# One-hot gates for eight tokens at a time, all on VectorE, with the stationary operand written token by token

## The chip, the cores and the metric

The kernel runs on one core of a Trainium2 chip. A core has engines that run beside one another, each with its own queue: TensorE (PE in the profile; its weight loads are PEld), VectorE (DVE), ScalarE (ACT), GpSimd (POOL) and SyncE (SP, which issues DMAs). The metric is the device time of one execution in microseconds (us). Three runs of the kernel before took 3183.05, 3179.83 and 3183.05 us; the median is 3183.05. [...]

## The reference

Two layers over 512 columns (256 latent tokens and 256 context tokens of 1024 features). Each layer has a mixer (a chunked gMLP in the first, a bidirectional S5 in the second) and then PEER, a layer of 16384 experts with one neuron each. The change touches PEER alone:

```python
def block(hb):                                   # 128 tokens
    q = (hb @ w_q).reshape(PEER_BLOCK, PEER_HEADS, 2, PEER_DHALF)
    s = jnp.einsum("nhkd,hkmd->nhkm", q, sub_keys)
    s_half, i_half = lax.top_k(s, PEER_TOPK)     # 16 of 128 keys, in both halves
    cand = s_half[:, :, 0, :, None] + s_half[:, :, 1, None, :]
    top_s, top_c = lax.top_k(cand.reshape(PEER_BLOCK, PEER_HEADS, 256), PEER_TOPK)
    k1 = jnp.take_along_axis(i_half[:, :, 0], top_c // PEER_TOPK, axis=-1)
    k2 = jnp.take_along_axis(i_half[:, :, 1], top_c % PEER_TOPK, axis=-1)
    ids = k1 * PEER_KEYS + k2
    g = jax.nn.softmax(top_s, axis=-1)
    act = jax.nn.gelu(jnp.einsum("nd,nhkd->nhk", hb, jnp.take(u_tab, ids, axis=0)))
    return jnp.einsum("nhk,nhkd->nd", g * act, jnp.take(v_tab, ids, axis=0))
```

So each token picks 8 heads x 16 = 128 experts (k1, k2), each with a gate g.

## The kernel before

PEER is not computed by gathering rows, but for the last 128 tokens of layer 0. For the other tokens (384 in layer 0, 256 in layer 1) the products with all 16384 experts are made, in 128 chunks of 128 experts, and the activations are multiplied by a matrix of gates that is zero where an expert was not chosen. A *front* (`front`, L695 on) loads a chunk of the U table, splits it into a high and a low part (`split`, L292: the high part on ScalarE, L296; the low part on VectorE or GpSimd, L298; tiles `uh` and `ul`), makes 24 TensorE products (L304 to L306) and applies GELU (L708). A *back* does the like with the V table.

The gate matrices are made by `gate_units` (L626), 128 tokens at a time, called a block below: three blocks in layer 0, two in layer 1. The 128 picks of a token lie on the 128 partitions after a transpose. For a group of 4 tokens VectorE compares a table of the numbers 0 to 127 (`iot`, each number four times, once per token) with the picks' k2 (L664, giving `o2`) and k1 (L666, giving `eq`), and multiplies `eq` by the gates. A gate is a sum of two float16 numbers, so there are two such products in `o1`: the upper one is made by VectorE (L668), the lower one (L669) by the engine `second`, which is GpSimd but for the third block of layer 0, where it is VectorE. In the tiles a token is the last index, so that a token's 128 places lie 8 bytes apart. TensorE then makes for each token o2^T times both halves of o1 (L653 and L654, two products with 128 stationary and 128 moving columns, both sides read in steps of 8 bytes), ScalarE copies a bank of four tokens to `Gs` (L655), and every 16 tokens a DMA writes 1 MB to DRAM, which the backs read.

There are 384/4 + 256/4 = 160 groups. The buffers `o2`, `eq` and `o1` have four copies each, and two groups' products are held back.

When this is done: in layer 0 the first 64 fronts, in layer 1 the first 68, are issued while `spread` moves the work of the routes (top-16 searches on VectorE) and of `gate_units` along, step by step; what is left is drained in `between()`, and the last two fronts of these come only after the last gate product (`ends["gates"]`). The order of the instructions on each engine is set by a scheduler from the program's order, its priorities and its own estimate of times; in layer 1 the low halves of the fronts go first (`HP`). The share of VectorE in the low halves of fronts is one in three in layer 0 and a half in layer 1.

Of the kernel before, what the change touches and what calls it, by code (L numbers as in the profile page):

```python
# [9 lines left out]
F32 = mybir.dt.float32  # L10
# [97 lines left out]
HG = 0  # L108


@with_exitstack
def tile_hybrid(ctx: ExitStack, tc: tile.TileContext, I, out, stop=None):
# [11 lines left out]
    def urgent(n):  # L124
        """A context of instructions that go before others."""
        return tc.high_priority(n) if n else ExitStack()
# [46 lines left out]
    def scale_cols(i, f, nf):  # L173
        """Norm gain times (1 + scale), for the blocks f..f+nf if they are a scale's."""
# [7 lines left out]
    def ada_pe(pa, f):  # L182
        """Shift, scale and gate of the first mixer on the tensor engine: rows, transposed to columns."""
# [22 lines left out]
    def ada_rows(pa, blocks, cB=None, e=nc.vector):  # L206
        """The other modulations as row products, a block of 128 features at a time, on engine e."""
# [29 lines left out]
    def rsqrt(v, r, y):  # L237
        """r = 1 / sqrt(v): a first value from the exponent's bits, refined by Newton steps."""
# [8 lines left out]
    def norm_add(pl, pm, b, t0, t1, e=nc.gpsimd):  # L247
        """Add block b's squares of the columns t0..t1: all but the last blocks' in a tile, then over the
        features, to the first columns of pm, with tokens on partitions."""
# [14 lines left out]
    def norm_end(pl, pm, n, r=None):  # L264
        """1 / sqrt(mean of squares + eps) on every partition; computed with tokens on partitions."""
# [26 lines left out]
    def split(hi, lo, src, dve=1, gps=1):  # L292
        """src (float32) as hi + lo, exactly, both in the format of one-pass products; the lower
        part by DVE and GpSimd in turn, in the given proportion."""
        turn[0] += 1
        nc.scalar.activation(hi, src, AF.Copy)  # L296
        e = nc.vector if turn[0] % (dve + gps) < dve else nc.gpsimd
        return e.tensor_tensor(lo, src, hi.bitcast(F32), op=OP.subtract)  # L298

    def mm3(o, pairs):  # L300
        """o = sum over pairs of lhsT^T rhs, each operand (hi, lo); lo times lo is below float32's rounding."""
# [7 lines left out]
    def modulate(pl, r, i, a, sh, parts, keep=None):  # L309
        """The normalised, modulated columns of XT as hi + lo, for parts (c, t0, t1, hi, lo); r from column parts[0].t0."""  # L310
# [14 lines left out]
    def residual(src, i, b, gate, part, view=lambda x: x):  # L325
        """XT block b += gate * src (columns as in XT)."""
# [8 lines left out]
    def gmlp(gw, hh, hl, r, vpump, vdone, upump, mid, pump):  # L335
        """Adds the mixer's output to XT; r = the norm of the result's columns."""
# [4 lines left out]
        with ExitStack() as st:  # L341
# [42 lines left out]
            def spatial(h):  # L384
# [10 lines left out]
                # the parts take the places of values that are no longer needed  # L395
# [16 lines left out]
            # the norm's gain and shift pass through the spatial product: gain * product + (shift * row sums + b_s)  # L412
# [43 lines left out]
    iot = cp.tile([P, KEYS, 4], F16, name="iot")  # L456
    nc.vector.tensor_copy(iot, i128.unsqueeze(2).to_broadcast([P, KEYS, 4]))
# [8 lines left out]
    def route(pr, S, gates, ids, kk, big={}):  # L466
        """Gates, both halves' keys and expert ids [P, heads, TOPK] from the scores [P, heads, 2, KEYS]."""
# [46 lines left out]
    # The score of a key is h . (w_q . key): the products of w_q with the keys come first.  # L514
    wp_d = [[dr.tile([P, KB, 512], F32, name=f"wp{i}_{q}") for q in range(4)] for i in range(2)]

    def wprime_units(pw, i, nb, e):
        """wp_d[i][pair of heads][d, block, (head, half, key)]; each step makes the products of one (head, half).
        e: the second engine of the copies."""
# [29 lines left out]
    def score_weights(i, pw, lo=(1, 2)):  # L549
        """The weights of scores, head by head, as (hi, lo)."""  # L550
# [9 lines left out]
    def scores(weights, ahead, pieces, S, done=lambda q: None):  # L560
        """S[block][token, head, half, key] from the pieces (hi, lo) of 128 tokens; ahead = weights already made."""
# [9 lines left out]
    def add_back(i, acc, a0, m, p0=0):  # L571
        """XT columns a0..a0+m += gate * acc, acc of [token, feature] from row p0."""
# [9 lines left out]
    # Experts of a token one by one: their rows are gathered.  # L582
    def gather_units(pg, i, hn, gates, ids, nh, finish, step=2):
        """Rows of the experts ids[:, head, slot], for nh heads; yields after `step` gathers; finish(acc)."""
# [35 lines left out]
    # All experts for the first n tokens: U^T chunks, GELU, gates (zero where an expert was not chosen), V chunks.  # L620
# [5 lines left out]
    def gate_units(pg, i, gates, kk, nt, g0, second):  # L626
        """gd[group, k2, k1, token] = the sum of the gates of expert (k1, k2), for nt tokens of a block. A gate
        is the sum of two float16, scaled by a power of two; places in a row are one-hot."""
        R = 4
        tr = pg.tile([P, 3, P], F32, name="jT", bufs=1)  # L630
# [3 lines left out]
        nc.scalar.copy(tr.rearrange("p q n -> p (q n)"), pm[:, 0:3 * P])  # L634
        kt = pg.tile([P, 2, P], F16, name="kt16", bufs=1)
        nc.vector.tensor_copy(kt, tr[:, 0:2])
        gt = pg.tile([P, 2, P], F16, name="gt16", bufs=1)
        gs = pg.tile([P, P], F32, name="gs", bufs=1)
        nc.vector.tensor_scalar(gs, tr[:, 2], GSCALE, None, op0=OP.mult)
# [3 lines left out]
        sh = [P, KEYS, R]  # L643
        pend = []

        def products(u, o1, o2):
            if u % (GT // R) == 0:
                Gs[0] = pg.tile([P, KEYS, GT], F32, name="Gs")
            n4 = u % (GT // R) * R
            pm = bank()  # L650
            for m in range(R):
                o = pm[:, m * P:(m + 1) * P]
                nc.tensor.matmul(o, o2[:, :, m], o1[:, 0, :, m], start=True, stop=False)  # L653
                ends["gates"] = nc.tensor.matmul(o, o2[:, :, m], o1[:, 1, :, m], start=False, stop=True).ins  # L654
# [6 lines left out]
        for u in range(nt // R):  # L661
# [890 lines left out]
```

## Time and profile before

| | before |
|---|---|
| median of three runs | 3183.05 us |
| the profiled execution: span | 3178.6 us |
| the profiled execution: a time of its own | none recorded; the three runs lie 1.2 to 4.5 us above the span |
| busy: PE, DVE, ACT, POOL | 2783.3, 2500.6, 1325.5, 1777.4 us |
| stretch of the gates in layer 0 | 680 to 1016 us |
| stretch of the gates in layer 1 | 2350 to 2616 us |

A busy time is the sum of the durations of an engine's instructions. The durations of successive instructions may overlap a little at the ends, so the distance from start to start is what an instruction really takes from its engine. In a row, L664 is the line of the program, and `o<-iot,kt` says which tile is written from which (o stands for both o1 and o2).

### The profile page before, as it was taken

The numbers are of one execution on the slowest core, as the hardware profiler recorded it, in microseconds if no ns is written. First come the engines' busy times: TensorE is split into PE (matmuls) and PEld (weight loads), VectorE is DVE, ScalarE is ACT, GpSimd is POOL, SyncE is SP. The second block draws the span as 40 slices with busy tenths as digits, with TensorE's granted clock in tenths as the row PEclk, the third lists the DMA queues.
The fourth block names the chain that finished last, engine by engine and source line by source line (L and its number), as shares of the span: only waits on it lengthen the run. The fifth ranks groups of instructions, "written<-read, shape, count | busy, mean of one in ns | idle before, by whom it ended". The sixth has DMA issues, their size and how long they took to land.

```text
span 3178.6 us, 46803 instructions
## 1 busy us (share of the span) xinstructions
PE 2783.3 (88%) x16231; PEld 2456.9 (77%) x16231; DVE 2500.6 (79%) x4335; ACT 1325.5 (42%) x2460; POOL 1777.4 (56%) x1228
## 2 busy tenths in 40 slices
PE   5789939888878888899999997988888789999998
PEld 1478839887867666688888875888888788889997
DVE  7992898999997887798999996764799986644444
ACT  3332343344436332333333322334344555555554
POOL 4581663566672444488888883135456655544443
PEclk8989969988988999999999998999899989999999
DMA  7548743545446878799999987998356668876663
GB/s 249 170 134 284 251 159 120 172 160 187 173 160 232 275 257 282 242 316 315 313 318 320 315 287 241 324 333 238 113 182 199 231 214 283 288 233 208 203 208 111
DMA packets 412534, 738.94 MB, mean 232 GB/s; under 512 B 41604, under 2 KB 270212, under 8 KB 407176
## 3 DMA queue, kind: packets, MB, share of 16 engines
q1 hardware_dynamic: 308192, 507.84, 48.2%
q0 software_dynamic: 36864, 134.23, 12.6%
q10 hardware_dynamic: 67240, 93.88, 8.3%
q8 instruction: 127, 2.08, 0.3%
q14 instruction: 111, 0.91, 0.1%
HBM read 633.07 MB, written 102.77 MB: 232 GB/s over the span
## 4 chain that ended last, share of the span: by engine, by line
PE 31%; DVE 13%; DMA 12%; issue 6%; POOL 4%; ACT 1%; SPq 1%; DVEq 0%; ACTq 0%; POOLq 0%
PE bk L744 5%; PE bk L745 5%; PE bk L743 5%; PE bk L306 4%; PE bk L304 4%; PE bk L305 4%; DMA vr<-peer_v 4%; POOL row L591 2%; DMA row<-peer_v,ids 2%; DMA wp<-wpo 1%; DVE ul L298 1%; POOL vl L298 1%; DVE o L668 1%; DVE acc L614 1%; DVE adasv L218 1%
## 5 line engine op out<-in xcount | busy, mean ns | idle before, releaser
L306 PE MATMUL bk<-hxh,ul 128*128 128x384 f32 (+1 forms) x2048 | 658.0, 322 | 36.4 <-DVE ul L298 23.5
L304 PE MATMUL bk<-hxh,uh 128*128 128x384 f32 (+1 forms) x2048 | 658.5, 322 | 13.3 <-ACT act L708 7.3
L305 PE MATMUL bk<-hxl,uh 128*128 128x384 f32 (+1 forms) x2048 | 651.9, 318 | 0.0
L298 POOL TENSOR_TENSOR vl<-vr,vh 128x512 fp32r<-128x512 f32 x256 | 360.7, 1413 | 456.4 <-ACT vh L296 452.8
L744 PE MATMUL bk<-vl,wh 128*128 128x512 f32 x1280 | 519.1, 406 | 59.7 <-POOL vl L298 41.7
L743 PE MATMUL bk<-vh,wh 128*128 128x512 f32 x1280 | 513.5, 401 | 30.9 <-ACT vh L296 20.4
L298 POOL TENSOR_TENSOR ul<-ur,uh 128x512 fp32r<-128x512 f32 x299 | 429.1, 1442 | 179.2 <-ACT uh L296 174.2
L296 ACT ACTIVATE vh<-vr 128x512 fp32r<-128x512 f32 x512 | 315.4, 623 | 500.4 <-DMA vr<-peer_v 362.1
L745 PE MATMUL bk<-vh,wl 128*128 128x512 f32 x1280 | 510.6, 399 | 0.0
L296 ACT ACTIVATE uh<-ur 128x512 fp32r<-128x512 f32 x512 | 314.5, 629 | 400.1 <-PE bk L305 217.8
L306 PEld LDWEIGHTS bk<-hxh,ul 128*128 128x128 f32 x2048 | 405.7, 198 | 42.7 <-DVE ul L298 28.2
L304 PEld LDWEIGHTS bk<-hxh,uh 128*128 128x128 f32 x2048 | 406.5, 198 | 20.8 <-ACT act L708 8.5
L305 PEld LDWEIGHTS bk<-hxl,uh 128*128 128x128 f32 x2048 | 405.4, 198 | 6.1 <-issue 0.9
L298 DVE TENSOR_TENSOR wl<-w,wh 128x384 fp32r<-128x384 f32 (+1 forms) x256 | 190.9, 746 | 239.4 <-ACT wh L296 239.2
L744 PEld LDWEIGHTS bk<-vl,wh 128*128 128x128 f32 x1280 | 247.9, 194 | 132.7 <-POOL vl L298 58.9
L743 PEld LDWEIGHTS bk<-vh,wh 128*128 128x128 f32 x1280 | 247.5, 193 | 86.3 <-ACT vh L296 26.0
L745 PEld LDWEIGHTS bk<-vh,wl 128*128 128x128 f32 x1280 | 247.7, 194 | 50.9
L298 DVE TENSOR_TENSOR vl<-vr,vh 128x512 fp32r<-128x512 f32 x256 | 204.1, 808 | 70.8 <-ACT vh L296 70.7
L614 DVE SCALAR_TENSOR_TENSOR acc<-row,wts,acc 128x1024 f32<-128x1024 f32 x127 | 211.5, 1665 | 24.9 <-DMA row<-peer_v,ids 23.6
L601 DVE SCALAR_TENSOR_TENSOR gscr<-row,hn 128x1024 f16<-128x1024 f32 x128 | 217.1, 1696 | 12.7 <-DMA row<-peer_u,ids 11.8
L298 DVE TENSOR_TENSOR ul<-ur,uh 128x512 fp32r<-128x512 f32 x213 | 192.3, 904 | 42.0 <-ACT uh L296 40.6
L653 PE MATMUL bk<-o,o 128*128 128x128 f16 x640 | 162.0, 296 | 70.1 <-DVE o L668 70.0
(344 smaller groups left out, 5753.0 us busy)
## 6 DMA issues: line engine op xcount, KB each, us to landing
ur<-peer_ut SPq DMA_DIRECT2D x256, 512.0 KB, 4.5
vr<-peer_v SPq DMA_DIRECT2D x256, 512.0 KB, 4.7
gd<-Gs ACTq DMA_DIRECT2D x40, 1024.0 KB, 4.1
wqT<-peer_w_q SPq DMA_DIRECT2D x64, 512.0 KB, 7.4
adatv<-ada_t SPq DMA_DIRECT2D x58, 512.0 KB, 5.6
Gr<-gd SPq DMA_DIRECT2D x120, 192.0 KB, 6.8
wp<-wpo ACTq DMA_DIRECT2D x32, 512.0 KB, 12.1
wpi<-wp SPq DMA_DIRECT2D x16, 1024.0 KB, 6.3
```

What stands on the lines that cost most here:

```text
L296: nc.scalar.activation(hi, src, AF.Copy)
L298: return e.tensor_tensor(lo, src, hi.bitcast(F32), op=OP.subtract)
L304: nc.tensor.matmul(o, ah, bh, start=(i == 0), stop=False)
L305: nc.tensor.matmul(o, ah, bl, start=False, stop=False)
L306: last = nc.tensor.matmul(o, al, bh, start=False, stop=(i == n - 1))
L591: tc.keep_in_program_order(nc.gpsimd.indirect_dma_start(out=r[:], out_offset=None, in_=I[f"peer_{table}{i}"], in_offset=bass.IndirectOffse ...
L601: nc.vector.scalar_tensor_tensor(scr, r, 1.0, hn, op0=OP.mult, op1=OP.mult, accum_out=dots[:, h, k:k + 1])
L614: nc.vector.scalar_tensor_tensor(acc, r, w, acc, op0=OP.mult, op1=OP.add)
L653: nc.tensor.matmul(o, o2[:, :, m], o1[:, 0, :, m], start=True, stop=False)
L743: nc.tensor.matmul(o, wh[:, js], vh, start=first, stop=False)
L744: nc.tensor.matmul(o, wh[:, js], vl, start=False, stop=False)
L745: nc.tensor.matmul(o, wl[:, js], vh, start=False, stop=last)
```

## The change

Eight tokens (`GR`) are treated at a time. `iot` has each number eight times, and with a second table `irow` (the numbers once) it is made in each layer, in the pool of the gates. Per eight tokens there is one comparison for `eq` (1024 elements a partition), eight comparisons of `irow` with the k2 of one token, a scalar on each partition, which write `o2` token by token so that its 128 places are contiguous, and one multiplication of 2048 elements for both halves of `o1`. All of it is on VectorE; the argument `second` is gone. A token's places in `o1` now lie 16 bytes apart. The copies out of the transposes are on ScalarE. `o2` and `o1` have three copies in layer 0 and two in layer 1, `eq` two. The rest of the diff is comments taken out, which also shifts the line numbers.

```diff
+GR = 8
...
-    iot = cp.tile([P, KEYS, 4], F16, name="iot")
-    nc.vector.tensor_copy(iot, i128.unsqueeze(2).to_broadcast([P, KEYS, 4]))
+
+    def places(pg):
+
+        iot = pg.tile([P, KEYS, GR], F16, name="iot", bufs=1)
+        nc.vector.tensor_copy(iot, i128.unsqueeze(2).to_broadcast([P, KEYS, GR]))
+        row = pg.tile([P, KEYS], F16, name="irow", bufs=1)
+        nc.vector.tensor_copy(row, i128)
+        return iot, row
...
-    def gate_units(pg, i, gates, kk, nt, g0, second):
+    def gate_units(pg, its, i, gates, kk, nt, g0):
...
-        tr = pg.tile([P, 3, P], F32, name="jT", bufs=1)
         pm = bank()
         for q, src in enumerate((kk[0], kk[1], gates)):
             nc.tensor.transpose(pm[:, q * P:(q + 1) * P], src.rearrange("p h k -> p (h k)"), ident)
-        nc.scalar.copy(tr.rearrange("p q n -> p (q n)"), pm[:, 0:3 * P])
-        kt = pg.tile([P, 2, P], F16, name="kt16", bufs=1)
-        nc.vector.tensor_copy(kt, tr[:, 0:2])
+        iot, row = its
+        kt = pg.tile([P, P], F16, name="kt16", bufs=1)
+        nc.scalar.copy(kt, pm[:, 0:P])
+        k2 = pg.tile([P, P], F32, name="k2t", bufs=1)
+        nc.scalar.copy(k2, pm[:, P:2 * P])
         gt = pg.tile([P, 2, P], F16, name="gt16", bufs=1)
         gs = pg.tile([P, P], F32, name="gs", bufs=1)
-        nc.vector.tensor_scalar(gs, tr[:, 2], GSCALE, None, op0=OP.mult)
+        nc.scalar.activation(gs, pm[:, 2 * P:3 * P], AF.Copy, scale=GSCALE)
...
-        sh = [P, KEYS, R]
+        sh = [P, 2, KEYS, GR]
...
             for m in range(R):
                 o = pm[:, m * P:(m + 1) * P]
-                nc.tensor.matmul(o, o2[:, :, m], o1[:, 0, :, m], start=True, stop=False)
-                ends["gates"] = nc.tensor.matmul(o, o2[:, :, m], o1[:, 1, :, m], start=False, stop=True).ins
+                k = u * R % GR + m
+                nc.tensor.matmul(o, o2[:, k], o1[:, 0, :, k], start=True, stop=False)
+                ends["gates"] = nc.tensor.matmul(o, o2[:, k], o1[:, 1, :, k], start=False, stop=True).ins
...
-        for u in range(nt // R):
-            ns = slice(u * R, u * R + R)
-            o2 = pg.tile(sh, F16, name="o2", bufs=4)
-            nc.vector.tensor_tensor(o2, iot, kt[:, 1, ns].unsqueeze(1).to_broadcast(sh), op=OP.is_equal)
-            eq = pg.tile(sh, F16, name="eq", bufs=4)
-            nc.vector.tensor_tensor(eq, iot, kt[:, 0, ns].unsqueeze(1).to_broadcast(sh), op=OP.is_equal)
-            o1 = pg.tile([P, 2] + sh[1:], F16, name="o1", bufs=4)
-            one = nc.vector.tensor_tensor(o1[:, 0], eq, gt[:, 0, ns].unsqueeze(1).to_broadcast(sh), op=OP.mult)
-            second.tensor_tensor(o1[:, 1], eq, gt[:, 1, ns].unsqueeze(1).to_broadcast(sh), op=OP.mult)
-            ends["places"] = one.ins
-            pend.append((u, o1, o2))
-            if len(pend) > 2:
-                products(*pend.pop(0))
-            yield
+        for v in range(nt // GR):
+            ns = slice(v * GR, (v + 1) * GR)
+            eq = pg.tile([P, KEYS, GR], F16, name="eq", bufs=2)
+            nc.vector.tensor_tensor(eq, iot, kt[:, ns].unsqueeze(1).to_broadcast([P, KEYS, GR]), op=OP.is_equal)
+            o2 = pg.tile([P, GR, KEYS], F16, name="o2", bufs=3 - i)
+            for k in range(GR):
+                nc.vector.tensor_scalar(o2[:, k], row, k2[:, v * GR + k:v * GR + k + 1], None, op0=OP.is_equal)
+            o1 = pg.tile(sh, F16, name="o1", bufs=3 - i)
+            nc.vector.tensor_tensor(o1, eq.unsqueeze(1).to_broadcast(sh), gt[:, :, ns].unsqueeze(2).to_broadcast(sh), op=OP.mult)
+            pend += [(v * GR // R + q, o1, o2) for q in range(GR // R)]
+            for _ in range(GR // R):
+                if len(pend) > 2:
+                    products(*pend.pop(0))
+                yield
...
-            ga = [gate_units(pt, 0, gk[j][0], gk[j][1], P, j * P // GT, nc.vector if j == 2 else nc.gpsimd) for j in range(3)]
+            its = places(pt)
+            ga = [gate_units(pt, its, 0, gk[j][0], gk[j][1], P, j * P // GT) for j in range(3)]
...
-            ga = [gate_units(pt, 1, gk[j][0], gk[j][1], P, j * P // GT, nc.gpsimd) for j in range(2)]
+            its = places(pt)
+            ga = [gate_units(pt, its, 1, gk[j][0], gk[j][1], P, j * P // GT) for j in range(2)]
```

How the order on the engines moves. On VectorE, in the first block of layer 0, where the routes' searches (MATCH_REPLACE, MAX) lie between the gate instructions; before:

```order
L666 TENSOR_TENSOR eq<-iot,kt_5470 128x512
L462 MATCH_REPLACE scr_5818<-tv,cand 128x256
L462 MATCH_REPLACE scr<-sv,S_3364 128x128
L664 TENSOR_TENSOR o_5739<-iot,kt_5470 128x512
L668 TENSOR_TENSOR o_5743<-eq,gt_5472 128x512
L463 MAX tv<-scr_5818 128x8
L664 TENSOR_TENSOR o_5800<-iot,kt_5470 128x512
L668 TENSOR_TENSOR o_5804<-eq,gt_5472 128x512
L463 MAX sv<-scr 128x8
```

and of the change, at the like place (x8 stands for eight in a row):

```order
L469 MATCH_REPLACE scr_5695<-tv,cand 128x256
L677 TENSOR_SCALAR o_5863<-irow,k2t 128x128 x8
L679 TENSOR_TENSOR o_5750<-eq,gt_5474 128x2048
L677 TENSOR_SCALAR o_5951<-irow,k2t 128x128
L679 TENSOR_TENSOR o_5872<-eq,gt_5474 128x2048
L677 TENSOR_SCALAR o_5951<-irow,k2t 128x128 x2
L470 MAX tv<-scr_5695 128x8
L677 TENSOR_SCALAR o_5951<-irow,k2t 128x128 x5
```

Where pairs of L664 and L668 stood for four tokens, runs of eight small comparisons and one large multiplication stand for eight.

On TensorE, at the third block of layer 0 (its transposes write bank 8552 before and 8521 after; L304 to L306, then L305 to L307, are the fronts' products). Before, the transposes are followed by products of the block ahead and by fronts, and the last front but two stands among the third block's products:

```order
L654 MATMUL bk_8446<-o_8409,o_8405 128x128
L633 MATMUL bk_8552<-ident,k_3351 128x128
L633 MATMUL bk_8552<-ident,gates_3349 128x128
L654 LDWEIGHTS o_8422
L654 MATMUL bk_8503<-o_8426,o_8422 128x128
```

```order
L304 MATMUL bk_9329<-hxh,uh 128x384
L305 MATMUL bk_9329<-hxl,uh 128x384
L306 MATMUL bk_9329<-hxh,ul 128x384
L653 LDWEIGHTS o_8767
L653 MATMUL bk_8847<-o_8771,o_8767 128x128
L654 LDWEIGHTS o_8767
L654 MATMUL bk_8847<-o_8771,o_8767 128x128
```

After that point come the block's last 192 products and no front but the last two. In the change that point is at the transposes themselves:

```order
L306 MATMUL bk_9291<-hxl,uh 128x384
L307 MATMUL bk_9291<-hxh,ul 128x384
L639 MATMUL bk_8521<-ident,k_3348 128x128
L639 MATMUL bk_8521<-ident,k_3349 128x128
L639 MATMUL bk_8521<-ident,gates_3347 128x128
L663 LDWEIGHTS o_8536
L663 MATMUL bk_8599<-o_8545,o_8536 128x128
L664 LDWEIGHTS o_8536
L664 MATMUL bk_8599<-o_8545,o_8536 128x128
```

All 256 products of the third block stand behind the last front but two.

## Rows read from the trace of the kernel before

**Rows 1.** Windows: length; busy us (count) of PE, PEld, DVE, ACT, POOL; clock; DMA; GB/s

```profile
680.00:1016.00 336.00, 283.91 (x1727) 260.93 (x1726) 317.38 (x695) 165.76 (x224) 203.03 (x154) 0.89 0.51 180
2350.00:2616.00 266.00, 222.02 (x1677) 210.84 (x1678) 252.03 (x434) 135.94 (x212) 164.31 (x116) 0.91 0.61 208
```

**Rows 2.** The same windows, tiles o alone: PE, PEld, DVE, POOL

```profile
680.00:1016.00 336.00, 108.59 (x768) 83.67 (x768) 136.87 (x224) 80.89 (x64) 0.89 0.51 180
2350.00:2616.00 266.00, 71.34 (x512) 53.93 (x512) 95.80 (x128) 81.86 (x64) 0.91 0.61 208
```

**Rows 3.** DVE by form, 680 to 1016: count, busy us, mean ns, idle before

```profile
L664 DVE TENSOR_TENSOR o<-iot,kt 128x512 f16<-128x512 f16 x96 | 69.4, 725 | 14.3 <-PE bk L654 14.3
L668 DVE TENSOR_TENSOR o<-eq,gt 128x512 f16<-128x512 f16 x96 | 64.2, 676 | 0.0
L666 DVE TENSOR_TENSOR eq<-iot,kt 128x512 f16<-128x512 f16 x96 | 55.8, 592 | 0.3 <-POOL o L669 0.3
L298 DVE TENSOR_TENSOR ul<-ur,uh 128x512 fp32r<-128x512 f32 x27 | 26.6, 985 | 0.0
```

**Rows 4.** DVE by form, 2350 to 2616

```profile
L668 DVE TENSOR_TENSOR o<-eq,gt 128x512 f16<-128x512 f16 x64 | 52.2, 820 | 0.0
L298 DVE TENSOR_TENSOR ul<-ur,uh 128x512 fp32r<-128x512 f32 x50 | 49.0, 980 | 1.9 <-ACT uh L296 1.9
L664 DVE TENSOR_TENSOR o<-iot,kt 128x512 f16<-128x512 f16 x64 | 48.6, 761 | 3.9 <-PE bk L654 3.9
L666 DVE TENSOR_TENSOR eq<-iot,kt 128x512 f16<-128x512 f16 x64 | 46.1, 732 | 1.2 <-POOL o L669 0.9
```

**Rows 5.** Timeline at 785 and at 2562 us: start, length, engine, line

```profile
785.33 0.41 DVE L668 TENSOR_TENSOR o<-eq,gt 128x512 f16<-128x512 f16 x1
...
786.00 0.41 DVE L668 TENSOR_TENSOR o<-eq,gt 128x512 f16<-128x512 f16 x1
...
2562.07 1.09 POOL L669 TENSOR_TENSOR o<-eq,gt 128x512 f16<-128x512 f16 x1 [0.42 <-DVE eq L666]
...
2562.19 1.26 DVE L668 TENSOR_TENSOR o<-eq,gt 128x512 f16<-128x512 f16 x1
```

**Rows 6.** Waits, 680 to 1016 us: total us, times, longest

```profile
PE bk L653 <- DVE o L668: 47.9, 29, 6.5
...
DVE o L664 <- PE bk L654: 14.3, 7, 5.0
```

**Rows 7.** Waits of DVE, 2420 to 2616 us

```profile
DVE o L664 <- PE bk L654: 3.9, 3, 2.5
```

**Rows 8.** Views by tile (gs, acc, ul): ns min/median/max, first and last start

```profile
L639 DVE TENSOR_SCALAR gs<-jT x5: 213/217/253, 679.1 to 2521.6; 128x128 f32<-128x128 f32 x5
...
L612 DVE TENSOR_SCALAR acc<-row,wts x1: 742/742/742, 1173.2 to 1173.2; 128x1024 f32<-128x1024 f32 x1
...
L298 DVE TENSOR_TENSOR ul<-ur,uh x213: 642/692/2885, 564.8 to 3124.5; 128x512 fp32r<-128x512 f32 x107
```

**Rows 9.** Timeline of PE, at 2571 and at 2563 us

```profile
2571.29 0.28 PE L304 MATMUL bk<-hxh,uh 128*128 128x256 f32 x1
2571.41 0.28 PE L305 MATMUL bk<-hxl,uh 128*128 128x256 f32 x1
...
2571.75 0.30 PE L653 MATMUL bk<-o,o 128*128 128x128 f16 x1
2571.87 0.30 PE L654 MATMUL bk<-o,o 128*128 128x128 f16 x1
...
2563.73 0.30 PE L653 MATMUL bk<-o,o 128*128 128x128 f16 x1
2563.85 0.30 PE L654 MATMUL bk<-o,o 128*128 128x128 f16 x1
```

**Rows 10.** Windows around these: columns as in rows 1

```profile
2571.20:2572.40 1.20, 1.20 (x12) 1.15 (x12) 0.00 (x0) 0.39 (x1) 0.00 (x0) 1.00 0.47 188
2562.00:2564.40 2.40, 0.90 (x8) 0.83 (x8) 2.40 (x5) 1.97 (x4) 1.57 (x2) 0.50 0.97 362
```

## The prediction

> **What bounds the kernel now.** I read four views, in this order. First the table of busy times of two stretches, those in which the gate matrices are built: 680 to 1016 us (layer 0, three blocks of 128 tokens) and 2350 to 2616 us (layer 1, two blocks) [rows 1]. What the reader should see: VectorE (DVE) is busy for 317 of 336 us and for 252 of 266, more than TensorE (284 and 222) and far more than GpSimd (POOL, 203 and 164). These 602 us are the only part of the span that the change touches, and DVE sets their length. Restricted to the gate tiles [rows 2], DVE spends 137 + 96 = 233 us there, POOL 81 + 82 = 163, and TensorE issues 768 and 512 of the gate products.
>
> Then the groups by form, which say why DVE needs so much [rows 3, 4]. The same instruction, 128x512 in float16, costs a mean of 592 to 820 ns. Alone it takes 0.41 us and the next starts 0.335 us after it (0.67 for two) [rows 5]. The last two rows there show what makes the difference: DVE's L668 starts 0.12 us after a GpSimd L669 and takes 1.26 us, ending 0.3 us after it. So DVE is stretched by the work that POOL does beside it.
>
> Last the list of waits [rows 6, 7]: DVE itself waits little, 14.3 and 3.9 us, for buffers that TensorE still reads; TensorE waits for DVE's L668 (47.9 us in layer 0). The order of command is DVE first, TensorE second.
>
> **The change, part by part.** There are 160 groups of 4 tokens now, so 80 of 8: 64 in the four blocks in which POOL makes the lower half of o1, 16 in the third block of layer 0, where DVE makes it.
>
> *Removed from DVE.* Per 8 tokens, six instructions (o2, eq, o1 high, twice) of 0.335 us are 2.01 us; in the third block eight are 2.68.
>
> *Added to DVE.* From the float16 row of 512 elements (0.41 us) and the float32 one with a constant of 128 (L639, 217 ns) [rows 5, 8] an element costs (410 - 217) / 384 = 0.50 ns, and the rest is fixed. So eq of 1024 elements takes 0.335 + 512 x 0.50 ns = 0.59 us from start to start, and o1 of 2048 takes 1.10. The eight comparisons of 128 elements with a scalar from memory have no row. L639 takes 217 ns, less the overlap of 0.08 that the gate rows show (0.41 against 0.335): 0.137. A scalar read from a column adds about 0.07: L612 takes 742 for 1024 elements, where 217 + 896 x 0.50 = 665. That is 0.207 if a comparison reads two values a step, as L639 does. All these rows agree with 8 bytes a step (two float32, or two pairs of float16), which for one float16 input would be four values: 32 steps of about 1 ns fewer, 0.174. One value a step would be 0.271. Eight of them: 1.39, 1.66 or 2.17. A group then costs 3.08, 3.35 or 3.86 us. Against before: 64 x 1.07 + 16 x 0.40 = +75 us; or +97; or +137. I take +75, since 8 bytes a step is what the nearest rows have in common, and keep the other two for the range. (That o1, with its two broadcast operands, runs as slowly as one value a step would add another 80 x 1 us; the existing o1 with the same kind of operand does not, so it is only in the far end.)
>
> *The tables and the copies.* The two index tables are made in each layer instead of once (a float16 of 1024 elements, 0.6 us at the rate above and perhaps three times that with a float32 source), and two small DVE instructions per block go to ScalarE, which is busy for half of either stretch and hides them. I take +2, between 0 and +4.
>
> *Removed from POOL.* All 128 L669 go. This is where a gain must come from: not from POOL's own time, which is no bound, but from DVE's stretching. Its size: in layer 0 the three gate groups are 96 x (0.725 + 0.676 + 0.592 - 3 x 0.41) = 73 us over their undisturbed time, the ul split 27 x (0.985 - 0.692) = 8 more; in layer 1 64 x (0.820 + 0.761 + 0.732 - 1.23) = 69 and 50 x (0.980 - 0.692) = 14 [rows 3, 4, 8]. That is 81 and 83. L669 is 81 of POOL's 203 busy us in the one stretch, 82 of 164 in the other [rows 1, 2], and the other POOL work stays. By these shares 0.40 x 81 + 0.50 x 83 = 74. The smaller two-input groups of DVE (routes, modulation) are stretched too and not in this; the upper end is 128 x 0.85 us (1.26 against 0.41, [rows 5]) = 109, each L669 blocking one instruction for its whole length. The lower end is 0, if POOL simply moves the splits that remain into the freed time and each of DVE's instructions meets one of these. I take -82, nearer to the shares than to the end.
>
> *Waits.* The 18 us in which DVE waits for a buffer of TensorE [rows 6, 7]: buffers now hold 3 x 8 tokens in layer 0 instead of 4 x 4, and 2 x 8 in layer 1, so the slack is at best a little larger. In layer 0 the order now puts all 256 products of the third block behind the last front (before, 64 of them lay between fronts), so TensorE has them to itself. I take half: -9, between 0 and -18. No new wait is added that is not there in another form: o2 and o1 are still waited for by the same products.
>
> *TensorE.* The same 1280 products. The stationary side is contiguous now; the moving side steps over 8 elements, 16 bytes, where it stepped over 8 bytes. The forecast holds these at their present 0.12 us each [rows 9]; both directions are rivals below.
>
> Sum: 75 + 2 - 82 - 9 = -14 us. The profiled execution's span is 3178.6, the runs lie 1.2 to 4.5 us above it, the median 4.4. So 3178.6 - 14 + 4.4 = 3169 us. By the bounds that do not belong to a rival (-18 for all of the waits, -95 for the stretch, or -74 and 0) this forecast's own range is 3152 to 3181.
>
> **Rivals.** *The moving side becomes the bound: slower.* At full granted clock 256 contiguous float32 columns take 0.12 us, and 128 float16 columns at 8-byte steps also 0.12; at half clock (0.50, 1.2 GHz) the latter still take 0.12 [rows 9, 10]. So a gate product is held by reading its operands, not by the array; which of the two operands holds it the trace cannot say, since both step alike now. If it is the moving one, and the cost goes with the bytes passed over, a product goes from 0.12 to 0.22. In layer 0 that is 768 x 0.105 = 81 us on 284, 365 against the 336 of the stage: +29. In layer 1 512 x 0.105 = 54 on 222, 276 against 266: +10. Together +39, or 3222 us. It decides from 0.185 us a product in layer 0 (52 us of room / 768) and 0.20 in layer 1 (44 / 512). For it: both sides of a product are read alike and nothing else explains the 0.12. Against: a weight load of the same stride is just as good a suspect. [...]
>
> *The comparisons cost more, and what POOL still does keeps stretching DVE: about even or a little slower.* At two values a step +97 + 2 - 82 - 9 = +8, 3191 us; with only three quarters of the stretch gone as well, +28 and 3211; with four values a step and three quarters gone, +6. For it: eight small instructions have eight times the fixed cost, and POOL keeps its splits of ul. Against: DVE's undisturbed rows. [...] No row shows a fast float16 instruction with one input beside POOL.
>
> *The contiguous weights are the gain.* If it is the stationary load that holds a product at 0.12, it falls to some 0.07, what 128 contiguous columns would take by half of the 256-column row. TensorE then has 1280 x 0.05 = 64 us less to do. DVE sets the pace, so only a part counts: the whole 18 us of waits instead of 9, and about half of the way to the upper end of the stretch (14), as blocks end earlier and fewer splits fall beside gates: -14 - 9 - 14 = -37, 3146 us.
>
> **Chances.** Forecast 0.40; moving side 0.22; even or a little slower 0.23; contiguous weights 0.15. A change is told from none here at about 0.2%, 6.4 us: below 3176.6 is faster, above 3189.4 slower. Forecast: 0.31 faster, 0.07 same, 0.02 slower. Moving side: 0.03 faster (0.14 us a product costs nothing), 0.02 same, 0.17 slower. Even: 0.01, 0.11, 0.11. Contiguous weights 0.15 faster. Together 0.50, 0.20, 0.30. The range goes from 3135 to 3222; half of the moving side's cases and a few below 3135 lie outside, some 0.15.
>
> **What the next profile should show.** The comparison at L677 at about 0.25 us, L674 0.67, L679 1.18, with means near their medians; above 0.28 at L677 the second rival is on. POOL's busy time down by 160 us. Start to start of the products: 0.12 for the forecast, over 0.18 for the first rival, under 0.09 for the third. The last gate product of layer 0 some 7 us earlier than now. Wrong: if DVE's gate tiles take over 270 us in sum, if the mean of the ul split stays near 0.98, or if TensorE, no longer DVE, is busy for all of a stage.

## The result, and the profile after

The changed kernel takes 3268.36 us (median of four runs, 3260.3 to 3272.09) against 3181.72 for the kernel before (3179.83 to 3183.05): a ratio of 1.0269, 95% interval 1.0254 to 1.0284. The forecast was 3169, a gain; measured is a loss of 87 us, 99 above the forecast. Its profiled execution has a span of 3270.3 us. One of e1's four runs below took 3217.6 us at a mean granted clock of 0.81 (TensorE's, as a share of its full speed), where its others had 0.93, and is left out.

The busy time of the two stretches, as in [rows 1] and with the same columns (length; busy us and count of PE, PEld, DVE, ACT, POOL; granted clock; DMA share; GB/s). They are longer now, so the windows reach to 1086 and 2720 us:

```profile
680.00:1086.00 406.00, 372.44 (x1719) 287.54 (x1718) 291.54 (x880) 170.10 (x227) 114.18 (x87) 0.76 0.40 147
2350.00:2720.00 370.00, 348.26 (x2247) 291.56 (x2246) 299.25 (x789) 182.79 (x296) 149.11 (x85) 0.89 0.58 199
```

TensorE is busy for 372 of 406 and 348 of 370 us, and VectorE no longer sets the pace (292 and 299). The granted clock of the first stretch fell from 0.89 to 0.76. The same windows for the gate tiles alone, which answer to [rows 2] (PE, PEld and DVE; POOL has nothing left):

```profile
680.00:1086.00 406.00, 178.69 (x768) 90.29 (x768) 135.41 (x432) 0.76 0.40 147
2350.00:2720.00 370.00, 123.00 (x512) 56.08 (x512) 87.94 (x288) 0.89 0.58 199
```

VectorE's groups by form in the first stretch (count, busy us, mean ns, idle before), for [rows 3], and its one wait for TensorE in the second, for [rows 7]:

```profile
L677 DVE TENSOR_SCALAR o<-irow,k2t 128x128 f16<-128x128 f16 x384 | 78.1, 270 | 70.2 <-PE bk L664 70.2
L679 DVE TENSOR_TENSOR o<-eq,gt 128x2048 f16<-128x2048 f16 x48 | 60.0, 1257 | 0.0
L674 DVE TENSOR_TENSOR eq<-iot,kt 128x1024 f16<-128x1024 f16 x48 | 32.6, 690 | 1.1 <-ACT kt L642 1.1
```

```profile
DVE o L677 <- PE bk L664: 45.6, 23, 4.3
```

In the first stretch the gate instructions of VectorE now run near their undisturbed length (690 ns where 682 is the median, 1257 where 1216 is); in the second L674 still has a mean of 934 ns. But VectorE stands for 70 and 46 us waiting for `o2` buffers that TensorE still reads; before these waits were 14 and 4 [rows 6, 7]. Why, three rows of TensorE's timeline show, among the third block's products (start, length):

```profile
1072.53 0.41 PE L663 MATMUL bk<-o,o 128*128 128x128 f16 x1
1072.76 0.41 PE L664 MATMUL bk<-o,o 128*128 128x128 f16 x1
1072.98 0.41 PE L663 MATMUL bk<-o,o 128*128 128x128 f16 x1
```

A gate product takes 0.227 us from start to start, where it took 0.118 [rows 9]. The last one starts at 1085.5 us in layer 0 and 2715.0 in layer 1, against 1013.6 and 2613.5 before: 72 us lost in layer 0, 30 more in layer 1, and some 10 given back from there to the end (565 us before, 555 now), for which no run here gives the cause.

### The profile page after: what moved, and what is told of

The parts are those of the page before. It is cut to its first block, busy times and chain, and to the rows that moved or that the text cites. A ratio compares the mean times of both kernels' runs of the same rounds, so it can differ in the third digit from the quotient of the medians.

```text
span 3270.3 us, 46840 instructions
## 1 busy us (share of the span) xinstructions
PE 2923.6 (89%) x16231; PEld 2489.4 (76%) x16231; DVE 2441.0 (75%) x4616; ACT 1337.4 (41%) x2470; POOL 1616.7 (49%) x1100
## 4 chain that ended last, share of the span: by engine, by line
PE 51%; DVE 22%; DMA 12%; issue 9%; POOL 4%; ACT 2%; SPq 1%; DVEq 0%; ACTq 0%; POOLq 0%
PE bk L307 8%; PE bk L306 8%; PE bk L305 8%; PE bk L754 5%; PE bk L755 5%; PE bk L753 5%; PE bk L663 4%; PE bk L664 4%; DMA vr<-peer_v 3%; DVE adasv L219 2%; DMA row<-peer_v,ids 2%; PE bk L551 2%; DMA row<-peer_u,ids 2%; POOL row L598 1%; DVE gscr L608 1%
## 5 line engine op out<-in xcount | busy, mean ns | idle before, releaser
L299 POOL TENSOR_TENSOR ul<-ur,uh 128x512 fp32r<-128x512 f32 x299 | 439.6, 1476 | 528.8 <-ACT uh L297 511.7
L307 PE MATMUL bk<-hxh,ul 128*128 128x384 f32 (+1 forms) x2048 | 664.7, 325 | 36.0 <-DVE ul L299 20.6
L305 PE MATMUL bk<-hxh,uh 128*128 128x384 f32 (+1 forms) x2048 | 667.1, 326 | 7.3 <-ACT uh L297 6.3
L306 PE MATMUL bk<-hxl,uh 128*128 128x384 f32 (+1 forms) x2048 | 660.8, 323 | 0.0
L307 PEld LDWEIGHTS bk<-hxh,ul 128*128 128x128 f32 x2048 | 411.2, 201 | 43.6 <-DVE ul L299 24.2
L305 PEld LDWEIGHTS bk<-hxh,uh 128*128 128x128 f32 x2048 | 412.4, 201 | 17.5 <-ACT uh L297 7.3
L306 PEld LDWEIGHTS bk<-hxl,uh 128*128 128x128 f32 x2048 | 411.9, 201 | 7.1
L663 PE MATMUL bk<-o,o 128*128 128x128 f16 x640 | 258.4, 404 | 11.0 <-DVE o L679 11.0
L664 PE MATMUL bk<-o,o 128*128 128x128 f16 x640 | 259.4, 405 | 0.0
L299 DVE TENSOR_TENSOR ul<-ur,uh 128x512 fp32r<-128x512 f32 x213 | 182.0, 855 | 82.3 <-ACT uh L297 81.8
L665 ACT ACTIVATE Gs<-bk 128x512 f32<-128x512 f32 x160 | 169.1, 1057 | 178.6 <-PE bk L664 175.4
```

Of the source, the lines that this page charges most:

```text
L305: nc.tensor.matmul(o, ah, bh, start=(i == 0), stop=False)
L306: nc.tensor.matmul(o, ah, bl, start=False, stop=False)
L307: last = nc.tensor.matmul(o, al, bh, start=False, stop=(i == n - 1))
L663: nc.tensor.matmul(o, o2[:, k], o1[:, 0, :, k], start=True, stop=False)
L664: ends["gates"] = nc.tensor.matmul(o, o2[:, k], o1[:, 1, :, k], start=False, stop=True).ins
L665: nc.scalar.activation(Gs[0][:, :, n4:n4 + R].rearrange("p k n -> p n k"), pm.rearrange("p (n k) -> p n k", n=R), AF.Copy, scale=1.0 / GSCALE)
```

## The experiments

Theory S: the moving side's 16-byte steps make the products slow, and TensorE's longer time is the loss. Rivals: O, the new order on the engines is the loss; V, VectorE's eight comparisons are; W, the stationary side's step counts as the moving one's does.

| run | us, median | ratio to the kernel before (95%) | us per product |
|---|---|---|---|
| the change | 3268.4 | 1.0269 (1.0254 to 1.0284) | 0.227 |
| e1 moving side contiguous | 3140.4 | 0.9859 (0.9826 to 0.9893) | 0.056 |
| e2 steps of 2, 4, 8, 16 bytes, moving | 3134.3 (one run) | | by step |
| e3 groups of four | 3148.6 | 0.9893 (0.9867 to 0.9918) | 0.116 |
| e4 before, all on VectorE | 3124.6 | 0.9818 (0.9793 to 0.9843) | 0.118 |
| e5 steps of 2 to 16 bytes, stationary | 3140.9 (one run) | | by step |
| e6 before, without the lower half | 3096.1 | 0.9735 (0.9698 to 0.9771) | 0.118 |
| e7 runs of four tokens | 3089.7 | 0.9709 (0.9689 to 0.9729) | 0.118 |
| e8 runs of two tokens | 3096.3 | 0.9718 (0.9694 to 0.9742) | 0.058 |
| f0 the change, 8-byte steps | 3134.3 | 0.9850 (0.9833 to 0.9866) | 0.116 |
| f1 f0, third block at 16 bytes | 3152.5 | 0.9907 (0.9891 to 0.9924) | both |
| f2 f0, blocks 1 and 2 at 16 bytes | 3209.6 | 1.0084 (1.0063 to 1.0106) | both |
| f3 f0, layer 1 at 16 bytes | 3182.8 | 1.0004 (0.9991 to 1.0016) | both |

**e1, the moving side contiguous.**

```diff
+c = [o1[:, h].rearrange("p n g -> p (n g)")[:, k * P:(k + 1) * P] for h in range(2)]
-nc.tensor.matmul(o, o2[:, k], o1[:, 0, :, k], start=True, stop=False)
+nc.tensor.matmul(o, o2[:, k], c[0], start=True, stop=False)
```

> The changed kernel, but TensorE reads the moving side of each gate product as 128 contiguous float16 instead of 128 at 16-byte steps (so the gates are wrong; every instruction and the order on TensorE, VectorE and ScalarE are those of the changed kernel). Theory S (the moving side's 16-byte steps hold a product at the 0.227 us from start to start that the changed kernel shows, and TensorE's 1280 x 0.109 us more is the loss): the distance falls to 0.06 to 0.12 us, and the time to about the forecast of 3169, between 3140 and 3190 us. Rival O (the new order is the loss: all fronts ahead of the third block of layer 0, which then waits for its routes and runs alone): the distance falls as well, but the time stays above 3215. Rival V (VectorE's comparisons are the loss): the time stays above 3250.

Measured 3140.4 us, 128 less than the change with the same instructions in the same order on every engine, at 0.056 us a product. S holds; O and V, as the whole of the loss, are out.

**e2, the step as the only variable.**

```diff
+s = (1, 2, 4, 8)[m]
+c = [o1[:, h].rearrange("p n g -> p (n g)")[:, 0:P * s].rearrange("p (n s) -> p n s", s=s)[:, :, k % s] for h in range(2)]
```

> The changed kernel, but the four products of a bank read their moving side at steps of 2, 4, 8 and 16 bytes, one step each (so the gates are wrong; the order is the changed kernel's). Theory S, with a cost that goes with the bytes passed over: 0.06 or less, 0.06, 0.12 and 0.227 us from start to start. [...] If the stationary load held the old products at 0.12: the 8-byte step is well below 0.12.

Eight products of one bank in TensorE's timeline, and the first of the next: two at each step from 2 bytes up (L665 and L666 are the two halves of a token). The granted clock there is 1.00, by the window below:

```profile
719.53 0.24 PE L665 MATMUL bk<-o,o 128*128 128x128 f16 x1
719.60 0.22 PE L666 MATMUL bk<-o,o 128*128 128x128 f16 x1
719.66 0.22 PE L665 MATMUL bk<-o,o 128*128 128x128 f16 x1
719.72 0.22 PE L666 MATMUL bk<-o,o 128*128 128x128 f16 x1
719.77 0.28 PE L665 MATMUL bk<-o,o 128*128 128x128 f16 x1
719.87 0.30 PE L666 MATMUL bk<-o,o 128*128 128x128 f16 x1
719.99 0.41 PE L665 MATMUL bk<-o,o 128*128 128x128 f16 x1
720.21 0.41 PE L666 MATMUL bk<-o,o 128*128 128x128 f16 x1
720.44 0.24 PE L665 MATMUL bk<-o,o 128*128 128x128 f16 x1
```

```profile
719.70:721.50 1.80, 1.80 (x20) 1.36 (x17) 1.80 (x10) 1.76 (x2) 0.00 (x0) 1.00 0.25 93
```

The reader should look at the distances between the starts of second halves and what follows: 0.06 at 2 bytes, 0.05 at 4, 0.12 at 8, 0.23 at 16. Over the whole run the medians are 0.056, 0.058, 0.117 and 0.227, most of them at this clock: 4-byte steps take 0.002 us more than the contiguous 0.056, 8 and 16 bytes about two and four times as long. The expectation of 8 bytes well below 0.12 is out. At a granted clock of 0.50 only the last step is much longer than the others. The same second halves, and the start after each, from 2 bytes up:

```profile
991.22 0.31 PE L666 MATMUL bk<-o,o 128*128 128x128 f16 x1
991.33 0.31 PE L665 MATMUL bk<-o,o 128*128 128x128 f16 x1
991.44 0.31 PE L666 MATMUL bk<-o,o 128*128 128x128 f16 x1
991.55 0.31 PE L665 MATMUL bk<-o,o 128*128 128x128 f16 x1
991.67 0.30 PE L666 MATMUL bk<-o,o 128*128 128x128 f16 x1
991.78 0.41 PE L665 MATMUL bk<-o,o 128*128 128x128 f16 x1
992.01 0.41 PE L666 MATMUL bk<-o,o 128*128 128x128 f16 x1
992.24 0.29 PE L665 MATMUL bk<-o,o 128*128 128x128 f16 x1
```

```profile
991.10:993.40 2.30, 2.26 (x16) 1.66 (x16) 2.30 (x9) 0.95 (x1) 0.00 (x0) 0.50 0.69 285
```

The distances are 0.11, 0.11, 0.11 and 0.23; in all such stretches of the run the medians are 0.107, 0.107, 0.118 and 0.227. The contiguous product nearly doubles at the lower clock (0.056 to 0.107), the two long steps take what they take at 1.00 (0.117 and 0.118 at 8 bytes, 0.227 at 16).

**e3, groups of four.** `GR = 4`, and twice the buffers.

> The changed kernel with groups of four tokens instead of eight and twice as many buffers: the moving side steps over 8 bytes as in the kernel before, the stationary side stays contiguous, all is still on VectorE, and TensorE's order in layer 0 still has the third block alone behind all fronts. Theory S: a product takes 0.12 us or less, the time is 3150 to 3195. Rival O: over 3215, since the order is the changed kernel's. Rival V: over 3250, VectorE has 3.17 us per eight tokens here where the changed kernel has 3.04.

3148.6 us with 0.116 us a product and TensorE's order unchanged in kind, as S said. It also answers for my third rival: the stationary side is contiguous here and the moving side at 8 bytes as before the change, and the product takes what it took before (0.116 us against 0.118). The contiguous weights give no more than these 0.002. Rival W needs e5.

**e4, the kernel before with line L669 on VectorE throughout.**

```diff
-P, j * P // GT, nc.vector if j == 2 else nc.gpsimd) for j in range(3)]
+P, j * P // GT, nc.vector) for j in range(3)]
```

> The kernel before with the lower half of the gates on VectorE in every block, so that GpSimd has none of it: the one part 'off GpSimd' alone. My step says 128 x 0.335 = 43 us more on VectorE against 82 us less stretching and about 9 us less waiting: 3135 us, between 3120 and 3160. Rival O (the third block's 256 products stand alone behind the fronts here too): that gain is eaten, 3180 to 3215. If GpSimd's remaining splits keep VectorE as stretched as before: 3215 to 3225.

3124.6 us, 57 faster than before, although VectorE has 43 us more to do. Its rows in the first stretch:

```profile
L664 DVE TENSOR_TENSOR o<-iot,kt 128x512 f16<-128x512 f16 x96 | 46.4, 491 | 0.0
L666 DVE TENSOR_TENSOR eq<-iot,kt 128x512 f16<-128x512 f16 x96 | 46.4, 508 | 0.0
...
L668 DVE TENSOR_TENSOR o<-eq,gt 128x512 f16<-128x512 f16 x96 | 43.0, 452 | 0.0
```

The means fell from 725, 592 and 676 ns [rows 3] to 491, 508 and 452, with GpSimd's splits still there, and the wait of 14 us for TensorE is gone in this stretch (in layer 1 it is 9.9 us, where it was 3.9). This is the step of my sum that the change was to gain from, and it is real.

**e5, the step of the stationary side** (moving side contiguous as in e1).

```diff
+s = (1, 2, 4, 8)[m]
+w = o2.rearrange("p g n -> p (g n)")[:, 0:P * s].rearrange("p (n s) -> p n s", s=s)[:, :, k % s]
```

> The changed kernel with the moving side contiguous and the stationary side of the four products of a bank read at steps of 2, 4, 8 and 16 bytes (so the gates are wrong; the order is the changed kernel's). Theory S says the moving side alone sets the distance: 0.056 us for all four, as with the contiguous moving side before. Rival W (a stationary load at a large step takes as long as a moving side at that step): 0.056, 0.058, 0.12 and 0.23 us.

Medians 0.056 at 2, 4 and 8 bytes, 0.063 to 0.067 around the loads at 16. W is out: even a load at the largest step adds at most 0.011 us, where the moving side's adds 0.171. (The order in which the trace shows these cannot tell which of two neighbours the last 10 ns belong to.)

**e6, the stretch by itself.**

```diff
-o1 = pg.tile([P, 2] + sh[1:], F16, name="o1", bufs=4)
-one = nc.vector.tensor_tensor(o1[:, 0], eq, gt[:, 0, ns].unsqueeze(1).to_broadcast(sh), op=OP.mult)
-second.tensor_tensor(o1[:, 1], eq, gt[:, 1, ns].unsqueeze(1).to_broadcast(sh), op=OP.mult)
+o1 = pg.tile(sh, F16, name="o1", bufs=4)
+one = nc.vector.tensor_tensor(o1, eq, gt[:, 0, ns].unsqueeze(1).to_broadcast(sh), op=OP.mult)
```

> The kernel before without the lower half of the gates: the 128 GpSimd and 32 VectorE instructions of line L669 are left out, and TensorE reads the upper half twice, so its work is unchanged. It prices the stretch: my step took 82 us for it, and 9 for waits. Against the kernel before with all of L669 on VectorE (3125 us; 128 instructions of 0.335 us more) this should be 43 + 11 (the 32 of the third block) = 54 us faster where VectorE sets the pace: 3070 us, 3055 to 3090, which would make the stretch about 95 us. If TensorE sets the pace there: 3105 to 3125.

3096.1 us: 87 less than before, where 82 + 9 + 11 = 102 follow from my sum, and 28.5 less than e4, where 54 were expected. Neither range held it. In its windows TensorE has become the busier engine, if by little in layer 0:

```profile
680.00:960.00 280.00, 263.98 (x1713) 254.75 (x1713) 260.03 (x678) 162.96 (x222) 125.76 (x86) 0.95 0.57 207
2350.00:2531.00 181.00, 169.38 (x1384) 165.09 (x1384) 156.52 (x291) 114.31 (x176) 61.70 (x39) 0.98 0.73 262
```

264 of 280 and 169 of 181 us against 260 and 157: VectorE no longer sets the pace alone, so the 87 us need not be all that it gave up.

**e7 and e8, versions of their own.** All four instructions per eight tokens are of 1024 elements on VectorE; the tokens lie in runs of four (8-byte steps) or two (4 bytes).

```diff
+sh = [P, GR // SUB, KEYS, SUB]
+nc.vector.tensor_tensor(o2, it, by(kt[:, 1, ns]), op=OP.is_equal)
+nc.vector.tensor_tensor(eq, it, by(kt[:, 0, ns]), op=OP.is_equal)
+for h in range(2):
+    nc.vector.tensor_tensor(o1[:, h], eq, by(gt[:, h, ns]), op=OP.mult)
...
+nc.tensor.matmul(o, o2[:, ka, :, kb], o1[:, 0, ka, :, kb], start=True, stop=False)
```

> A new version: eight tokens at a time on VectorE, all four instructions of 1024 elements and no comparison with a scalar, tokens in runs of four, so that both sides of a product step over 8 bytes. VectorE needs 4 x 0.60 = 2.40 us per eight tokens, against 2.69 in the kernel before with all on VectorE and 3.17 with groups of four and scalar comparisons; TensorE 0.117 a product. If VectorE sets the pace: 3125 less up to 23, so 3100 to 3115 us. If TensorE does: 3120 to 3130.

> The same with tokens in runs of two: both sides step over 4 bytes. Theory S: a product takes 0.058 us, TensorE has 75 us less to do, VectorE 2.40 us per eight tokens: 3060 to 3105 us, with VectorE as the bound. Rival: VectorE reads runs of two float16 at one value a step: 4 x 1.1 = 4.5 us per eight tokens, 150 us more, over 3200 us.

3089.7 and 3096.3 us: e7 is the fastest kernel here, 2.9% under the kernel before, a larger gain than the 3100 to 3115 expected. Halving the product's time again (e8) gains nothing. Windows of the first stretch, e7 and then e8:

```profile
680.00:957.00 277.00, 258.65 (x1700) 247.17 (x1699) 270.29 (x568) 162.53 (x224) 132.44 (x86) 0.95 0.57 208
```

```profile
680.00:963.00 283.00, 237.86 (x1728) 223.12 (x1727) 276.60 (x593) 160.94 (x226) 140.57 (x88) 0.92 0.58 209
```

VectorE is busy for 270 of 277 us in e7, TensorE for 259; in e8 TensorE's 21 us less leave VectorE at 277 of 283. VectorE's instructions of 1024 elements take the same 0.602 us from start to start in both, so the rival of e8 is out.

**f0 to f3: what the slow products cost, block by block.** All four have the change's order; `cond` picks the blocks that read at 16 bytes.

```diff
+s = 8 if cond else 4
+c = [o1[:, h].rearrange("p n g -> p (n g)")[:, 0:P * s].rearrange("p (n s) -> p n s", s=s)[:, :, k % s] for h in range(2)]
```

> The changed kernel and its order, but every gate product reads its moving side at 8-byte steps (so the gates are wrong): the base for the three that follow. From the group of four (8-byte steps, 3149 us, with 0.13 us more of VectorE per eight tokens): 3135 to 3150 us, 0.117 us a product. If the price of the steps has no other cause, 3268 less this is what all 1280 products at 16 bytes cost, near 1280 x 0.11 = 141 us if nothing of it lies beside other work.

> As the base, but the 256 products of the third block of layer 0, which stand alone behind the fronts, read at 16-byte steps (0.227 us): 28 us more of TensorE. Theory R (my rival's room: TensorE fills its idle time before the stage grows): 9 us more than the base, since the block's VectorE time is 16 x 3.04 = 49 us and its products would take 58. Theory N (no room: what TensorE gets more goes into the time one to one): 25 to 30 us more.

> As the base, but the 512 products of the first two blocks of layer 0 at 16-byte steps: 56 us more of TensorE, beside fronts and routes. Theory R: 56 less some 50 of idle time, 5 to 15 us more than the base. Theory N: 50 to 60 more, and above that if the fronts between them get a lower granted clock than in the base.

> As the base, but the 512 products of layer 1 at 16-byte steps: 56 us more of TensorE. Theory R: 56 less some 24 to 47 of idle time, 10 to 30 us more than the base. Theory N: 45 to 60 more, less what the later fronts, which are issued in the meantime, give back.

Against f0 (3134.3 us): third block +18, the first two +75, layer 1 +48; together 141, and the change itself is 134 above f0. TensorE's longer products are 28, 56 and 56 us. So the third block comes between the two theories, layer 1 is at theory N, and the first two blocks cost more than TensorE's extra time. f0 shows why there was little room, in windows of 80 us (the last of 82):

```profile
680.00:760.00 80.00, 76.62 (x500) 74.40 (x499) 80.00 (x224) 43.99 (x61) 30.88 (x20) 0.96 0.63 221
760.00:840.00 80.00, 73.65 (x424) 72.23 (x422) 79.52 (x244) 35.66 (x59) 41.81 (x28) 0.96 0.53 184
840.00:920.00 80.00, 77.22 (x509) 74.68 (x508) 80.00 (x191) 47.10 (x65) 34.34 (x22) 0.98 0.55 202
920.00:1002.00 82.00, 38.40 (x301) 33.40 (x300) 74.94 (x228) 37.30 (x43) 14.07 (x19) 0.63 0.35 135
```

and its waits of TensorE in 680 to 1002:

```profile
PE bk L665 <- DVE o L681: 26.3, 17, 7.1
PE bk L639 <- DVE k L509: 24.5, 4, 17.3
```

Of TensorE's 56 idle us in the stage, 44 stand in the last window, where it waits for the third block's routes (21.8 of the 24.5) and for the gate tiles of VectorE (21.8 of the 26.3); beside the products of the first two blocks there were 12. And f2's first three windows:

```profile
680.00:760.00 80.00, 76.68 (x350) 58.79 (x349) 57.14 (x179) 34.25 (x44) 19.70 (x13) 0.77 0.43 155
760.00:840.00 80.00, 80.00 (x396) 69.24 (x395) 53.57 (x171) 35.91 (x53) 31.55 (x22) 0.89 0.46 165
840.00:920.00 80.00, 74.21 (x345) 62.20 (x344) 65.49 (x194) 29.55 (x46) 27.45 (x19) 0.83 0.45 160
```

The granted clock is 0.77 to 0.89 where f0 has 0.96 to 0.98, with TensorE as busy; what lowered it, no run here takes apart. The fronts pay for it. From the first front to the last gate product of layer 0 both runs make the same 1488 front products, and these hold TensorE (from each start to the next, or to its end where TensorE then stands) for 304 us in f2 and 280 in f0. That stretch is 70 us longer in f2: 54 of longer gate products and 24 of slower fronts, less 8 of idle time. These 70 are most of f2's 75.

f0 also shows what the splits left on GpSimd do to the small comparisons: VectorE's group in 680 to 1002, eight comparisons in a row, and the two splits beside them.

```profile
L679 DVE TENSOR_SCALAR o<-irow,k2t 128x128 f16<-128x128 f16 x384 | 99.2, 334 | 0.0
```

```profile
690.98 3.10 DVE L679 TENSOR_SCALAR o<-irow,k2t 128x128 f16<-128x128 f16 x8
690.57 1.31 POOL L299 TENSOR_TENSOR ul<-ur,uh 128x512 fp32r<-128x512 f32 x1 [3.14 <-ACT uh L297]
692.43 1.27 POOL L299 TENSOR_TENSOR ul<-ur,uh 128x512 fp32r<-128x512 f32 x1 [0.56 <-ACT uh L297]
```

Undisturbed, eight take 1.39 us in the change; here they take 3.10. Of f0's 640 comparisons 55 take over one and a half times the median of 0.246 us, all of them while GpSimd works, and 46 of these end about 0.05 us after a split does. Together they are 57 us over their median (13 in the change).

## Why the prediction was wrong

**The step that failed** is the one headed TensorE: "The forecast holds these at their present 0.12 us each". They take 0.227, as the first rival had it (0.22), because of the moving side's 16-byte steps alone (e1, e2, e5). With them at 0.116 the change would have been faster: f0 is 3134 us, 0.9850 of the kernel before.

**What I chose badly.** From the rows (0.12 us at a granted clock of 1.00 and of 0.50 alike [rows 9, 10]) I had concluded that a product is held by reading its operands. Against the moving side stood only that the weight load was as good a suspect, and I gave that the greater weight: 0.22 for the moving side, 0.78 for everything else. The trace of before could not settle it: it has gate products at 8-byte steps alone. e2 does. At a granted clock of 1.00 a product takes 0.056 us contiguous, 0.058 at 4-byte steps, 0.117 at 8 and 0.227 at 16: the cost begins between 4 and 8 bytes and doubles from 8 to 16. At 0.50 the 8-byte step takes 0.118 against 0.107 contiguous, and the 16-byte one 0.227.

**The rival's price was too low**: 3222 against 3268. It had the products' 81 + 54 us about right (gate products hold TensorE for 169 and 108 us in the change, 91 and 59 before), but took off 52 and 44 us of TensorE's idle time as room. Up to the last gate product of layer 0 TensorE still idles for 34 us in the change: in f0 most of the idle time stands where the third block's routes and tiles are awaited. The fronts at the lower granted clock took more (24 us in f2). "No new wait is added" was wrong too: VectorE's waits for TensorE grew from 18 to 116 us.

**The signs I had named.** Products over 0.18 us and TensorE busy for nearly all of a stage (372 of 406 us) said that the first rival had come. The comparison's median (0.247 us), GpSimd's busy time (1777.4 to 1616.7 us, 161 less) and VectorE's 223 us of gate tiles are as forecast. The mean of the ul split, another sign, fell to 0.878 us in layer 0 and stayed at 0.984 in layer 1. My own range of 3152 to 3181 is not what its bounds add up to: that is 3147 to 3186.

**Right, by the runs.** The cost of a group on VectorE: 0.602 + 8 x 0.163 + 1.136 = 3.04 us, where the sum had 3.08; the comparison's 0.163 is nearest to the 0.174 that I chose, below the 0.207 that I kept for the range. The values a step from which I worked out these two were my estimate; the run shows the time alone. The second rival's dearer comparisons did not come; that what GpSimd still does stretches them did, in f0 (mean 0.334 us in layer 0); in the change few met a split so, and the mean stayed under my sign of 0.28 (0.270). The 1.2 GHz that I put beside a clock of 0.50 stands in no view; what the trace of before shows there is 1.2 contiguous float32 columns a ns (384 in 0.320 us from start to start, 256 in 0.213).

**Right in kind, off in size.** The stretch and the waits: -91 in my sum. e4 gives 57 + 43 = 100, e6 gives 87 - 11 = 76. That GpSimd's L669 stretched VectorE is shown by e4: in sum, VectorE's gate instructions stood 140 us over their medians before and 59 in e4, with the lower halves among them. With both terms as forecast, f0 should have been at 3169 and is at 3134, 35 us below. Only some 3 us of that is the group's cost; for the rest I have no run that prices it by itself. One part can be read: in layer 1 the sum puts VectorE's extra 34 us (32 groups at 1.07) wholly on the path, where in f0 TensorE and VectorE are about level (211 and 217 us of the 228 from 2350 to 2578).

**The third rival** (contiguous weights are the gain) is false: by e3 and e5 the stationary side's step up to 8 bytes costs nothing (0.056 us at 2, 4 and 8).

## What to carry to other kernels

When a tile's layout is changed for one reader, work out the step for every other reader, and price the moving operand of TensorE by it, at the clock that the stretch is granted: at 1.00 a step of 8 bytes took the 128-column float16 product from 0.056 to 0.117 us, at 0.50 from 0.107 to 0.118 (e2). Before counting an engine's idle time as room, look at where in the stage it lies. Taking work off GpSimd, whose instructions ran beside VectorE's, paid over twice what it cost VectorE (e4, 100 us for 43); with the layout left at 8-byte steps and large instructions instead of many small ones (e7), the idea of this change is worth 2.9%, of which the move alone gives 1.8% (e4).

## What the runs showed of the hardware that I had not expected

- The moving operand of a 128-column float16 product: 0.056 us contiguous, 0.058 at 4-byte steps, 0.117 at 8, 0.227 at 16, at a granted clock of 1.00; 0.107, 0.107, 0.118 and 0.227 at 0.50 (e2).
- The stationary load's step: the distance stays at 0.056 us up to 8 bytes, and 16 add under 0.012 (e5).
- A float16 comparison of 128 elements with a column's scalar takes 0.163 us from start to start on VectorE, and instructions of 1024 elements in runs of two the same 0.602 as in runs of eight (e8).
- Of the 640 comparisons of this kind in f0, 46 long ones lasted until about 0.05 us after the end of a GpSimd split, at a median of 0.246 us for all.
- The windows of 80 us in which TensorE issues products at 16-byte steps were granted a lower clock than the like ones at 8-byte steps: 0.77 to 0.89 against 0.96 to 0.98, at 74 to 80 us busy against 74 to 77 (f2, f0).
